# A memory-bound SwiGLU: the first tile loaded in three parts, and multiplied and stored in eight column pieces

## The chip, the cores and the metric

One core of a Trainium2 chip. The metric is the device time of the kernel in microseconds (us); lower is better. All runs quoted here were with the clock granted in full (1.00 in every one). A trace's span is some 1.8 us shorter than the time of its run. ACT is ScalarE, DVE VectorE; SP is SyncE, which here only issues transfers. A transfer (DMA) is cut into packets, here one for each contiguous row (in the kernel before 3968 loads of 64 KB and 3840 stores of 32 KB, besides those of the last two tiles), and 16 DMA engines carry them (16.0 packets are under way at a time, on the mean from 100 to 900 us). A transfer has landed when its last packet has arrived. "Packet records" are the start, length and size of each packet in a trace; sums over them are given for one engine, as the mean of the 16.

## The reference

```python
# x: 8192 x 8192 float32
a, b = np.split(x, 2, axis=-1)
return a * (b / (1 + np.exp(-b)))      # 8192 x 4096 float32
```

The input is 268.4 MB and the output 134.2 MB. All of it passes through the DMA engines once (402.67 MB in the trace of the kernel before).

## The kernel before

Two rows of x lie in one partition, so a tile is 128 partitions x 16384 floats (64 KB in each partition, 8 MB in all). There are 32 tiles and three buffers. ACT computes silu in place, DVE multiplies in place, and the product lies packed in the first half of the tile. SP issues the loads, ACT the stores, but those of the last two tiles are issued by SP.

```python
def load(i, rows=None):
    if i not in tiles:
        tiles[i] = pool.tile([P, R * M], x.dtype, name="xt")
    lo, hi = (0, R) if rows is None else rows
    nc.sync.dma_start(
        out=tiles[i][:, lo * M : hi * M], in_=xv[i * P : (i + 1) * P, lo * M : hi * M]
    )

def swiglu(i, k, c0=0, cw=half):
    xt = tiles[i]
    b = xt[:, k * M + half + c0 : k * M + half + c0 + cw]
    nc.scalar.activation(out=b, in_=b, func=_SILU)
    nc.vector.tensor_mul(out=xt[:, k * half + c0 : ...], in0=xt[:, k * M + c0 : ...], in1=b)

def store(i, c0=0, cw=R * half):
    (nc.scalar if i < last - 1 else nc.sync).dma_start(
        out=ov[i * P : (i + 1) * P, c0 : c0 + cw], in_=tiles[i][:, c0 : c0 + cw]
    )

for i in range(BUFS):            # 3
    load(i)
for i in range(last):            # 31
    for k in range(R):           # 2
        swiglu(i, k)
    if i == last - 1:
        swiglu(last, 0)
    store(i)
    nxt = i + BUFS
    if nxt < last:
        load(nxt)
    ...                          # the last tile: loaded, computed and stored by rows
```

## Time and profile before

| | before |
|---|---|
| time, median of 6 runs | 936.4 us (935.6 to 937.1) |
| span of the trace | 934.8 us |
| busy DVE, ACT | 30%, 25% |
| mean rate, whole span | 431 GB/s |
| mean rate, 100 to 900 us | 434 GB/s |
| load: issue to landing | 34.5 us |
| store: issue to landing | 39.7 us |
| period of a tile | 29.0 us |

A tile brings 8 MB in and 4 MB out, 12.58 MB in 29.0 us, which is the 434 GB/s. The compute engines idle for two thirds of the time and nothing is wrong with that: they are not the bound. The DMA engines are (9 tenths or more busy in 39 of 40 slices). The two landing times are longer than the 29 us period because each queue holds a little more than one transfer at a time (34.5/29.0 = 1.2 loads, 39.7/29.0 = 1.4 stores). Of a load's 34.5 us its own packets take 19.3 in each engine (8 x 2.418), of a store's 39.7 us 9.7 (8 x 1.213); the rest is time spent waiting in line.

In steady state the three buffers go round in a ring: load 34.5, compute 12.7, store 39.7, together 87 us, three periods.

### The profile page before, as it was taken

What the parts mean: (1) busy time and instruction counts of PE and PEld (TensorE: products, weight loads), DVE (VectorE), ACT (ScalarE), POOL (GpSimd) and SP (SyncE); (2) the same over time, 40 slices, a digit from 0 to 9 for tenths busy, and PEclk for the clock granted to TensorE, in tenths of its full rate; (3) what the DMA queues carried; (4) which work ended last, traced back from release to release, by engine and by line L of the source; (5) the groups of instructions that cost most, each with busy time, mean ns of one, the idle gap of its engine ahead of it and who ended that gap; (6) DMA issues with size and microseconds to landing.
All of it is one profiled execution on the core that took longest, in us unless ns stands there. A gap on an engine that the chain in (4) does not pass through costs nothing.

```text
span 934.8 us, 367 instructions
## 1 busy us (share of the span) xinstructions
DVE 283.3 (30%) x65; ACT 229.4 (25%) x66; POOL 0.2 (0%) x4
## 2 busy tenths in 40 slices
DVE  0333312333123331133321333213332133331242
ACT  0223320233302333113331133311333203332041
POOL 0000000000000000000000000000000000000000
DMA  9999999999999999999999999999999999999998
GB/s 404 400 445 430 430 439 433 428 435 443 428 430 439 429 442 432 435 426 453 419 430 452 411 452 423 428 447 425 433 433 453 414 443 429 426 447 428 425 437 376
DMA packets 9506, 402.67 MB, mean 431 GB/s; under 512 B 1056, under 2 KB 1056, under 8 KB 1056
## 3 DMA queue, kind: packets, MB, share of 16 engines
q1 hardware_dynamic: 5184, 276.83, 68.6%
q10 hardware_dynamic: 4320, 125.83, 31.2%
q14 instruction: 2, 0.02, 0.0%
HBM read 268.44 MB, written 134.22 MB: 431 GB/s over the span
## 4 chain that ended last, share of the span: by engine, by line
DMA 84%; DVE 10%; ACT 4%; DVEq 0%; issue 0%; SPq 0%; ACTq 0%
DMA out_dram<-xt 42%; DMA xt<-in_x_dram 42%; DVE xt L51 10%; ACT xt L50 4%; DVEq L106 0%; SPq L43 0%; ACTq L50 0%; DVEq L51 0%
## 5 line engine op out<-in xcount | busy, mean ns | idle before, releaser
L51 DVE TENSOR_TENSOR xt<-xt 128x4096 f32<-128x4096 f32 (+1 forms) x65 | 283.3, 4359 | 637.7 <-ACT xt L50 634.5
L50 ACT ACTIVATE xt<-xt 128x4096 f32<-128x4096 f32 (+1 forms) x65 | 228.1, 3556 | 688.1 <-DMA xt<-in_x_dram 688.1
L50 ACT ACT_TABLE_LOAD x1 | 1.3, 1283 | 0.7 <-PEq L95 0.7
L95 POOL MEMSET const-bfloat16-1.0<- 128x1 bf16 x1 | 0.1, 103 | 0.0
L95 POOL MEMSET const-uint8-127<- 128x1 uint8 x1 | 0.1, 102 | 0.0
L95 POOL MEMSET const-float32-0.0<- 128x1 f32 x1 | 0.1, 100 | 0.2 <-issue 0.2
L95 POOL MEMSET const-float32-1.0<- 128x1 f32 x1 | 0.1, 99 | 0.0
## 6 DMA issues: line engine op xcount, KB each, us to landing
out_dram<-xt ACTq DMA_DIRECT2D x30, 4096.0 KB, 39.7
xt<-in_x_dram SPq DMA_DIRECT2D x2, 4096.0 KB, 27.1
out_dram<-xt SPq DMA_DIRECT2D x1, 4096.0 KB, 23.6
out_dram<-xt SPq DMA_DIRECT2D x2, 2048.0 KB, 14.5
xt<-in_x_dram SPq DMA_DIRECT2D x31, 34.5
```

Of the source, the lines that this page charges most:

```text
L50: nc.scalar.activation(out=b, in_=b, func=_SILU)
L51: nc.vector.tensor_mul(out=xt[:, k * half + c0 : k * half + c0 + cw], in0=xt[:, k * M + c0 : k * M + c0 + cw], in1=b,)
L95: nc = _bacc.Bacc("TRN2", target_bir_lowering=False, num_devices=1)
```

## The change

Nothing is written in the first 35 us: the first tile has to arrive whole (it is there at 22.6 us) and be computed (12.6 us) before its store. The change loads tile 0 as a piece of 1024 columns of both halves of row 0 (1 MB), the rest of row 0 (3 MB) and row 1 (4 MB), and computes and stores it in eight pieces of 1024 columns.

```diff
+    def load_piece(i, k, c0, cw):
+        if i not in tiles:
+            tiles[i] = pool.tile([P, R * M], x.dtype, name="xt")
+        src = xv[i * P : (i + 1) * P, :].rearrange("p (k s c) -> p k s c", k=R, s=2)
+        dst = tiles[i].rearrange("p (k s c) -> p k s c", k=R, s=2)
+        nc.sync.dma_start(out=dst[:, k, :, c0 : c0 + cw], in_=src[:, k, :, c0 : c0 + cw])
...
-    for i in range(BUFS):
+    q = half // 4
+    load_piece(0, 0, 0, q)
+    load_piece(0, 0, q, half - q)
+    load(0, (1, 2))
+    for i in range(1, BUFS):
         load(i)
     for i in range(last):
+        step = q if i == 0 else half
         for k in range(R):
-            swiglu(i, k)
+            for c0 in range(0, half, step):
+                swiglu(i, k, c0, step)
+                if i == 0:
+                    store(i, k * half + c0, step)
         if i == last - 1:
             swiglu(last, 0)
-        store(i)
+        if i:
+            store(i)
```

## The prediction

> **What bounds the kernel now.** I read the page first: engine shares, then the 40 slices, then the queues.
>
> ```profile
> DVE 283.3 (30%) x65; ACT 229.4 (25%) x66; POOL 0.2 (0%) x4
> ...
> DMA  9999999999999999999999999999999999999998
> ...
> q1 hardware_dynamic: 5184, 276.83, 68.6%
> q10 hardware_dynamic: 4320, 125.83, 31.2%
> ...
> HBM read 268.44 MB, written 134.22 MB: 431 GB/s over the span
> ```
>
> No compute engine is busy for a third of the span, while the 16 DMA engines are at 9 tenths in every slice but the last. The two queues (q1: the loads and the last stores, issued by SP; q10: the other stores, issued by ACT) take 99.8% of the DMA time. So the limit is the bytes, 402.7 MB, and a change can help only by filling moments in which the DMA engines idle or run slowly. How many there are is read from the windows (columns: stretch, its length, DVE and ACT busy, POOL, clock, DMA share, GB/s):
>
> ```profile
> 22.00:36.00 14.00, 8.85 (x2) 7.12 (x2) 0.00 (x0) 1.00 0.93 403
> 36.00:60.00 24.00, 8.85 (x2) 7.12 (x2) 0.00 (x0) 1.00 1.05 429
> 60.00:100.00 40.00, 8.85 (x2) 7.12 (x2) 0.00 (x0) 1.00 0.97 422
> 100.00:500.00 400.00, 123.91 (x28) 99.72 (x28) 0.00 (x0) 1.00 1.00 435
> 500.00:900.00 400.00, 123.31 (x28) 99.72 (x28) 0.00 (x0) 1.00 1.00 433
> 900.00:932.00 32.00, 9.51 (x4) 7.33 (x3) 0.00 (x0) 1.00 0.99 428
> 932.00:935.00 3.00, 0.00 (x0) 0.00 (x0) 0.00 (x0) 1.00 0.07 27
> ```
>
> A packet here is a whole row of 64 or 32 KB and is counted in one piece, so windows of a few us are off by some per cent; long ones are good. From 100 to 900 us the mean is 434 GB/s, and 402.65 MB at that rate take 927.8 us. The span is 934.8, so only 7.0 us are lost in all. The window from 0 to 100 us has 418 GB/s: 16 GB/s too few for 100 us is 1.6 MB, or 3.7 us at 434. From 900 to 932 it is 6 GB/s x 32 us = 0.19 MB, 0.4 us; after 932 there is almost nothing, 2.8 us. **The whole of the start, which is all that the change touches, thus has 3.7 us to give, 0.4% of the time.** The packet records of the trace say what these are: the first packet starts 1.74 us into the span; the first packet of each engine takes about 3.1 us where a 64 KB packet later takes 2.42; and where the first store joins (36 to 42 us) one or two load packets of each engine take 3 to 4 us.
>
> The timeline shows when stores begin:
>
> ```profile
> 22.61 7.12 ACT L50 ACTIVATE xt<-xt 128x4096 f32<-128x4096 f32 x2 [20.60 <-DMA xt<-in_x_dram]
> 26.25 8.96 DVE L51 TENSOR_TENSOR xt<-xt 128x4096 f32<-128x4096 f32 x2 [26.25 <-ACT xt L50]
> 35.24 0.37 ACTq L58 DMA_DIRECT2D out_dram<-xt  x1
> ```
>
> Nothing is written before 35 us. It looks like waste and isn't: in that time loads of tiles 1 and 2 are already queued and keep the engines full. A 64 KB load packet takes 2.42 us both alone (10 to 35 us) and between stores (after 100 us): 27.1 GB/s an engine, 434 GB/s for 16. Reads alone run as fast as reads and writes mixed.
>
> [...] with both queues filled an engine takes one load packet (2.42 us) and one store packet (1.21 us) in turn, one round each 3.62 us. [...] The change's first load is 1 MiB and its first eight stores 0.5 MiB each; no transfer of this size is in the trace of before. The records do bound the fixed part: two 32 KB packets (2 x 1.213) against one of 64 KB (2.418) differ by 8 ns.
>
> **The change part by part.**
> Removed: one 8 MB load, four operations on 4096 columns and one 4 MB store, all of tile 0.
> Added: loads of 1 MB (16 packets of 4 KB an engine), 3 MB (16 of 12 KB) and 4 MB (8 of 32 KB); eight operations of 1024 columns on ACT and on DVE; eight stores of 8 packets of 4 KB. Bytes are the same. Packets an engine: 8 + 8 become 40 + 64, 88 more; at 8 ns that is 0.7 us. If they cost twice that, 1.4 us.
> ACT: from 3.61 us at 4096 and 1.90 at 2048 columns, 0.19 fixed + 0.855 per 1024, so 1.05 us a piece; DVE (4.425 and 2.288) 0.15 + 1.07 = 1.22 us. The order on ACT is silu, store, silu, store; a store waits for its multiply, so a piece takes about 2.4 us, eight take 19 instead of 12.6. Neither engine is the bound, so this is hidden.
> Moved, worked with packet times (about 0.16 us for 4 KB, 0.46 for 12 KB, 1.21 for 32 KB, 2.42 for 64 KB): the first piece has landed near 6 us, its store is issued near 8.3 instead of 35.2. The 3 MB piece lands near 14, store 1 is issued near 16.6. From here each 4 KB store packet waits behind a load packet: row 1 until about 24.5 us (1.37 us a round), then tile 1 (2.58 a round, 8 rounds, until 45), then tile 2 (until 66). Store 1 ends near 32, store 2 near 53, and at 66 some 35 small packets of tile 0's stores are left, which alone take 35 x 0.16 = 5.6 us, until about 71.5.
> The built program shows two waits made by the reuse of eight DMA semaphores: tile 2's load now waits for store 1 (near 33 us: 12 us before tile 1's load runs out, so no gap), and tile 1's store for store 2 (near 54, before its data are ready at 59). Tile 3's load waits for all eight stores, so it is issued near 73; before, it was at 69.9. In between, tile 1's store (issued near 59, queued behind the pieces) keeps the engines busy from 71.5. From 75 us loads and stores alternate as before.
> Sum: no DMA idle time removed except perhaps part of the 3.7 us, 0.7 to 1.4 us of packet overhead added, and the 1 to 1.5 us stall at the first store kept or had once more, since the store queue runs empty after store 0. Net: about +0.5 us.
>
> **The rivals.**
> (a) Overlap gain: stores begin 27 us earlier, and if those 27 us had been unused for writing, 27 us would be won at the end. Against it: the DMA share is 0.9 to 1.0 from the start and the rate is at its plateau; bytes written early only push back bytes read. It would give 910 us; I don't believe it. A small part of it, an end to the slow packets of the start, gives 933.
> (b) Starvation: tile 0's buffer comes free later because small packets lose every turn, the loads run dry at 66 us and SP waits until 73. For it: the rounds above. Against harm: while loads are missing, stores are queued (tile 0's rest, then 4 MB of tile 1), and the engines work on. Only if pieces of 4 KB ran at half speed alone would it cost: 8.4 MB touched by the change, 19 us at full rate, but only the 2.6 us of the first load and the 5.6 us of the rest stand alone: +8 us, 944. If the semaphore waits also opened a gap, 948.
> (c) Shifted phase at the end: with reads and writes displaced by some us, the last tile could find an emptier store queue, and its last multiply (landing 914.5, last store issued 921.0) would be exposed. The queues have slack: load 34.5 us and store 39.7 us to landing in a 29 us period. Worth 1 to 3 us at most.
>
> **Range and chances.** 936.4 + 0.5 gives 936.9; call it 937. Low 933.5: most of the 3.7 us recovered. High 941.5: half of rival (b). The 2% marks are 18.7 us off: a gain so large is five times what the start holds, a loss so large needs 8.1 MB worth of DMA idleness. Faster 0.005, same 0.97, slower 0.025.
>
> **What would show it.** Right: store issues from about 8 us on; the third 8 MB load (tile 3's) near 73 us; DMA 9 in all slices but the last, about 415 to 420 GB/s in the first 100 us; 434 after; tile 0's stores taking 15 to 45 us to landing though each is only 0.5 MB. Wrong: a slice of DMA under 9 between 60 and 80 us (b), a rate clearly over 434 in any long window (a), or a gap after 915 us (c).

The sum came to about +0.5 us (0.7 to 1.4 us of packets, less perhaps part of the 3.7 us): 936.9, called 937. No window of 400 us that was taken of these runs has more than 435 GB/s.

The packet times of the forecast, 0.16 us for 4 KB and 0.46 for 12 KB, are estimates from the 2.418 us of 64 KB and the 8 ns a packet; the trace of the changed kernel has 0.159 and 0.460. That a piece gets one packet's turn was an estimate too, from the turns in the trace of before (from 100 to 900 us, one load packet of an engine follows the last after 3.62 us in the median, and in 73% of the cases). The changed kernel shows it for the pieces: one 4 KB store packet and one 32 KB load packet in turn take 1.36 us, beside a 64 KB one 2.57. The eight semaphores are in both traces, the transfers land on eight. The half speed in rival (b) is an assumption; in e5_small_packets (below) 4 KB reads alone moved 370 to 393 GB/s from 10 to 40 us, not half of 434.

## The result, and the profile after

937.1 us (936.6 to 938.5, 6 runs) against 936.4: the ratio is 1.001 with a 95% interval of 0.9997 to 1.0023. A ratio here is the mean time of one kernel's fast runs over that of the other's fast runs of the same rounds, so it isn't quite the ratio of the medians. **The time did not change.** The stores did start early. The timeline of the changed kernel (start, length, engine, line, operation; the idle time before it in brackets):

```profile
6.42 1.06 ACT L58 ACTIVATE xt<-xt 128x1024 f32<-128x1024 f32 x1 [4.41 <-DMA xt<-in_x_dram]
7.50 1.23 DVE L59 TENSOR_TENSOR xt<-xt 128x1024 f32<-128x1024 f32 x1 [7.50 <-ACT xt L58]
8.76 0.37 ACTq L66 DMA_DIRECT2D out_dram<-xt  x1
...
36.35 0.34 ACTq L66 DMA_DIRECT2D out_dram<-xt  x1
46.51 7.12 ACT L58 ACTIVATE xt<-xt 128x4096 f32<-128x4096 f32 x2 [11.44 <-DMA xt<-in_x_dram]
...
68.13 7.12 ACT L58 ACTIVATE xt<-xt 128x4096 f32<-128x4096 f32 x2 [14.50 <-DMA xt<-in_x_dram]
```

The first store is issued at 8.8 us instead of 35.2 and the eighth at 36.4. Tile 1 is there at 46.5 us, as before (46.4). The windows of the changed kernel (stretch, length, DVE, ACT, POOL, clock, DMA share, GB/s):

```profile
0.00:100.00 100.00, 27.50 (x12) 23.98 (x13) 0.20 (x4) 1.00 0.99 418
100.00:500.00 400.00, 123.91 (x28) 99.72 (x28) 0.00 (x0) 1.00 1.00 435
500.00:900.00 400.00, 119.49 (x27) 99.71 (x28) 0.00 (x0) 1.00 1.00 433
```

The kernel before, for the first of these stretches:

```profile
0.00:100.00 100.00, 26.55 (x6) 22.65 (x7) 0.20 (x4) 1.00 0.99 418
```

Set beside the kernel before: 418 GB/s in the first 100 us in both, 435 and 433 after that in both. 26 us of earlier writing have moved not one more byte by the time 100 us have passed. What was written early was read later. Counted from the packet records, the kernel before has read 11.89 MB and written nothing at 30 us; the changed one has read 10.65 and written 0.82. At 100 us the sums are 41.62 and 41.50 MB.

What did change is in the page of the changed kernel, its chain and its issues (size, us from issue to landing):

```profile
DMA xt<-in_x_dram 49%; DMA out_dram<-xt 35%; DVE xt L59 10%; ACT xt L58 4%; DVEq L124 0%; SPq L51 0%; SPq L45 0%; ACTq L58 0%; DVEq L59 0%
...
out_dram<-xt ACTq DMA_DIRECT2D x29, 4096.0 KB, 32.3
...
out_dram<-xt ACTq DMA_DIRECT2D x8, 512.0 KB, 37.1
...
xt<-in_x_dram SPq DMA_DIRECT2D x30, 41.9
```

The issues of the kernel before, and of a version with a later first store (e6_store_later, below):

```profile
out_dram<-xt ACTq DMA_DIRECT2D x30, 4096.0 KB, 39.7
xt<-in_x_dram SPq DMA_DIRECT2D x31, 34.5
```

```profile
out_dram<-xt ACTq DMA_DIRECT2D x30, 4096.0 KB, 33.7
xt<-in_x_dram SPq DMA_DIRECT2D x31, 40.5
```

Before, the chain had 42% for each direction, loads took 34.5 us to landing and stores 39.7. Now loads take 41.9 and stores 32.3. The sum is 74.2 in both. In the changed kernel 7.4 us of waiting stand in the load queue and no longer in the store queue, for the whole rest of the run, and the period stayed 29 us. This isn't the mark of an early store: a first store that comes 7 or 19 us later (e3_store_late: loads 40.0, stores 34.3; e6_store_later: 40.5 and 33.7) or a split load alone (e1_load_split: 39.9 and 34.4) shifts it the same way, and the sum stays at 74.2 to 74.3. How the 74 us divide is decided somewhere at the start; what decides it, these runs don't settle, and no time goes with it. A reader who looked at the store alone would see a store that had become 19% faster, in a kernel that hadn't.

The 512 KB line is worth a look too: an eighth of a tile took as long to store (37.1 us) as a whole tile did (39.7 in the kernel before). Beside a filled load queue each small packet waited behind a large load packet (one 4 KB and one 64 KB packet in turn, 2.57 us a round, from 24 to 42 us), and each piece behind the pieces before it (they landed in order of issue, from 23.5 to 72.7 us). In c2_hold_change (below) four of the same pieces were issued when no load was queued; they landed in 2.6 to 2.9 us.

### The profile page after: what moved, and what is told of

Its sections match the earlier page's. It is cut to its first block, busy times and chain, and to the rows that moved or that the text cites. A ratio compares the mean times of both kernels' runs of the same rounds, so it can differ in the third digit from the quotient of the medians.

```text
span 936.7 us, 400 instructions
## 1 busy us (share of the span) xinstructions
DVE 284.2 (30%) x71; ACT 230.7 (25%) x72; POOL 0.2 (0%) x4
## 4 chain that ended last, share of the span: by engine, by line
DMA 84%; DVE 10%; ACT 4%; DVEq 0%; issue 0%; SPq 0%; ACTq 0%
DMA xt<-in_x_dram 49%; DMA out_dram<-xt 35%; DVE xt L59 10%; ACT xt L58 4%; DVEq L124 0%; SPq L51 0%; SPq L45 0%; ACTq L58 0%; DVEq L59 0%
## 5 line engine op out<-in xcount | busy, mean ns | idle before, releaser
L59 DVE TENSOR_TENSOR xt<-xt 128x4096 f32<-128x4096 f32 (+2 forms) x71 | 284.2, 4005 | 638.1 <-ACT xt L58 635.0
L58 ACT ACTIVATE xt<-xt 128x4096 f32<-128x4096 f32 (+2 forms) x71 | 229.5, 3273 | 688.2 <-DMA xt<-in_x_dram 679.8
## 6 DMA issues: line engine op xcount, KB each, us to landing
out_dram<-xt ACTq DMA_DIRECT2D x29, 4096.0 KB, 32.3
out_dram<-xt ACTq DMA_DIRECT2D x8, 512.0 KB, 37.1
xt<-in_x_dram SPq DMA_DIRECT2D x30, 41.9
```

The lines of the kernel that those rows point to most:

```text
L59: nc.vector.tensor_mul(out=xt[:, k * half + c0 : k * half + c0 + cw], in0=xt[:, k * M + c0 : k * M + c0 + cw], in1=b,)
```

## The experiments

The theory (A): the 16 DMA engines work without a hole from the first packet on, at one rate whether they read or write, so that the time is bytes over rate plus a start and an end; when writing starts doesn't matter. The rivals: (B) the early start gains something which the small pieces give back, so that the parts of the change alone would differ from 1 in opposite directions; (C) reading and writing overlap, so that the start of writing matters by itself.

| run | what | us | before, same rounds | ratio, 95% |
|---|---|---|---|---|
| e1_load_split | load split only | 936.6 | 936.3 | 1.0004 (0.9991 to 1.0016) |
| e2_store_split | store split only | 936.3 | 936.3 | 1.0000 (0.9987 to 1.0012) |
| e4_rows | the change in large pieces | 937.8 | 936.3 | 1.0018 (1.0005 to 1.0030) |
| e3_store_late | first store 7 us later | 936.4 | 936.3 | 1.0002 (0.9989 to 1.0016) |
| e6_store_later | first store 19 us later | 935.9 | 936.5 | 0.9993 (0.9977 to 1.0010) |
| c1_hold | a hole at the start | 956.4 | 936.5 | 1.0211 (1.0194 to 1.0228) |
| c2_hold_change | that hole, with the change | 948.0 | 936.5 | 1.0125 (1.0110 to 1.0140) |
| c3_hold_sp | a cleaner hole | 951.3 | 936.5 | 1.0159 (1.0142 to 1.0176) |
| c4_hold_sp_change | that hole, with the change | 937.8 | 936.5 | 1.0018 (1.0003 to 1.0033) |
| e5_small_packets | all packets 4 KB | 991.8 | 936.5 | 1.0601 (1.0576 to 1.0625) |
| f1_change_again | the change once more | 937.3 | 936.3 | 1.0011 (0.9997 to 1.0025) |

All gave correct results.

### The parts of the change, one by one

**e1_load_split**, against the changed kernel:

```diff
-        step = q if i == 0 else half
+        step = half
-                if i == 0:
-                    store(i, k * half + c0, step)
-        if i:
-            store(i)
+        store(i)
```

> Only the load of tile 0 is split (1 MB, 3 MB, 4 MB); it is computed in two halves of 4096 columns and stored whole, as before. Theory A (the DMA engines are busy from the first packet, so only packet overhead and stalls count): the store starts near 36 us as before, with its stall of 1.5 us; 40 load packets for 8 in each engine add about 0.25 us, slow small first packets 0.3 us: 936.4 + 0.5, ratio 1.000 to 1.002. Rival B (the early load gains time which the small stores give back): under 0.998.

**e2_store_split**, against the changed kernel:

```diff
-    load_piece(0, 0, 0, q)
-    load_piece(0, 0, q, half - q)
-    load(0, (1, 2))
-    for i in range(1, BUFS):
+    for i in range(BUFS):
         load(i)
```

> Tile 0 is loaded whole as before, but multiplied and stored in eight pieces from about 25 us. Theory A: 56 more store packets at 8 ns add 0.45 us, the stall where the first store joins may shrink from 1.5 to about 0.3 us as it did in the changed kernel: 935.5 to 937, ratio 0.999 to 1.001. Rival B (small stores cost several us, hidden in the changed kernel by a gain of the early start): 1.003 or more.

Measured: 1.0004 and 1.0000. Each part alone is worth nothing: neither the small loads nor the small stores cost anything that a gain would have to make good, at the level of 0.15% that these intervals resolve. Neither part has the whole early start, though (the first store is issued at 31.9 us in the first, at 25.1 in the second); the next run has it, without small packets.

**e4_rows**, against the changed kernel:

```diff
-    load_piece(0, 0, 0, q)
-    load_piece(0, 0, q, half - q)
+    load(0, (0, 1))
     load(0, (1, 2))
...
-        step = q if i == 0 else half
+        step = half
```

> The change with large pieces: tile 0 is loaded as two rows of 4 MB and stored as two rows of 2 MB, no packet under 16 KB (the store rows are 16 KB, the loads 32 KB). Theory A: packet overhead is under 0.15 us; the stores start near 22 us instead of 35, which gains nothing: 935.5 to 937, ratio 0.999 to 1.001. Rival B (an early start is worth something once the small packets are gone): under 0.996.

Measured: 937.8, 1.0018, so 0.8 us above the range I gave. Its first store is issued at 21.0 us, and it isn't faster, so rival B falls. But it is slower by 1.5 us without a small packet in it. At 900 us it is 0.25 MB (0.6 us) behind the kernel before. In its packet records the load packets from 24 to 36 us, where the stores join, took 1.1 us longer in each engine than the usual 2.42 us each, and those from 76 to 84 us, where loads start again after their queue had run empty, another 0.7 us. The kernel before has 1.5 us of the first kind, at 36 to 44 us, and none of the second; the changed kernel has 0.3 and 0.4. Why load packets are slow when one of the two queues starts, and why by so different amounts, these runs don't settle. Nor is the rest of the 1.5 us accounted for (0.4 of it lies after the last packet, 1.6 us before the span's end against 1.2 in the kernel before).

### The start of writing, moved the other way

**e3_store_late**, against the kernel before:

```diff
             swiglu(i, k)
         if i == last - 1:
             swiglu(last, 0)
+        if i == 0:
+            continue
+        if i == 1:
+            store(0)
+            load(BUFS)
         store(i)
```

> The opposite of the change: tile 0's store is issued only with tile 1's, near 59 us instead of 35. Theory A: reads fill the engines until 60 us, then two queued stores; tile 3's load waits for the first store, issued near 71 instead of 70: nothing lost, ratio 0.998 to 1.002. Rival C (the time at which writing starts matters, as reads and writes overlap): 24 us later costs up to 24 us, ratio 1.01 to 1.026.

The edit did less than I meant. Its timeline shows the store beside the first activation of tile 1, at 42.0 us, not at 59: the store waits for a multiply that was long done (at 35.3 us), and it was issued as the first of tile 1's two activations started.

```profile
42.01 3.62 ACT L50 ACTIVATE xt<-xt 128x4096 f32<-128x4096 f32 x1 [12.20 <-DMA xt<-in_x_dram]
42.01 0.37 ACTq L58 DMA_DIRECT2D out_dram<-xt  x1
```

So this is a delay of 6.8 us. Rival C would have it cost up to 0.7%; measured 1.0002 with an upper end of 1.0016. To make it larger, **e6_store_later** put tile 0's store behind tile 1's:

```diff
-        store(i)
+        if i == 0:
+            continue
+        if i == 1:
+            store(1)
+            store(0)
+            load(BUFS)
+        else:
+            store(i)
```

> Tile 0's store is issued behind tile 1's, near 55 us (the first attempt moved it only from 35 to 42, since ACT issued it beside the first activation of tile 1). Theory A: reads fill the engines until about 59 us, two stores from 56 to 78, tile 2's from 75: ratio 0.998 to 1.003. Rival C (the time at which writing starts matters): 20 us later, up to 1.021.

The timeline shows both stores together, 19 us later than the first store of the kernel before:

```profile
45.60 8.96 DVE L51 TENSOR_TENSOR xt<-xt 128x4096 f32<-128x4096 f32 x2 [10.37 <-ACT xt L50]
54.59 0.86 ACTq L58 DMA_DIRECT2D out_dram<-xt  x2
64.83 7.12 ACT L50 ACTIVATE xt<-xt 128x4096 f32<-128x4096 f32 x2 [15.75 <-DMA xt<-in_x_dram]
```

The time is 935.9 us, ratio 0.9993. Writing started at 9 us, at 35 or at 55 us, and the kernel took the same time (937.1, 936.4 and 935.9 us). Rival C falls. Meanwhile the reads run ahead: tile 2 is there at 64.8 us, 10.6 us earlier than in the kernel before (75.4).

### What would make the change pay

If A is right, the change must pay in a kernel whose DMA engines do idle at the start. So I made one: the loads of tiles 1 and 2 held back behind tile 0's store. **c1_hold**, against the kernel before (`load` gets an argument for the issuing engine):

```diff
-    for i in range(BUFS):
-        load(i)
+    load(0)
...
         store(i)
+        if i == 0:
+            load(1, eng=nc.scalar)
+            load(2, eng=nc.scalar)
```

> A control, the kernel before with an artificial hole: the loads of tiles 1 and 2 are issued by ACT behind tile 0's store, at about 36 us, so the DMA engines idle from about 22.5 to 37 us. Theory A (time follows the DMA engines' idle time): 14.5 us longer, 951, ratio 1.0155. Rival (there is slack in the three buffers that takes such a hole up): under 1.005.

**c2_hold_change** is the changed kernel with the same hold, the two loads issued by ACT behind the eight stores.

> The same hole with the change in it: tile 0 in pieces, tiles 1 and 2 loaded behind its eight stores. Theory A: by the time the loads are issued (about 37 us) 12.6 MB are through instead of 8.4, so 4.2 MB or 9.7 us of the hole are filled, less 0.8 us of packet overhead: 942 to 944, ratio 1.006 to 1.008 to before, some 8 us under the control. Rival (small stores run slowly or block the queue): no better than the control.

Measured: 956.4 and 948.0. The difference, 8.4 us, is what was expected, but both are some 5 us longer than expected. The windows of c1_hold say where:

```profile
22.00:37.00 15.00, 8.85 (x2) 7.12 (x2) 0.00 (x0) 1.00 0.08 35
37.00:96.00 59.00, 8.57 (x2) 7.12 (x2) 0.00 (x0) 1.00 1.02 435
96.00:150.00 54.00, 17.98 (x5) 15.68 (x5) 0.00 (x0) 1.00 0.95 385
```

There is the hole that I made, 35 GB/s from 22 to 37 us, and a second, 385 GB/s from 96 to 150: 49 GB/s too few for 54 us is 2.6 MB, or 6 us at 434 (5.4 us by the packet records). I made that one too, by mistake. Tile 3's load, issued by SP at 47 us, shared the engines with those of tiles 1 and 2 in ACT's queue and overtook tile 2's (its packets ended at 86 us, tile 2's at 106). Tile 1's store stood behind tile 2's load in ACT's queue and was through at 116 us. At that time tiles 2 and 3 were both still in compute, and nothing was queued until tile 4's load, issued at 116 us. By the packet records the engines idled for 2.0 us there; the other 3.4 us are load packets slower than 2.42 us around it (100 to 132 us). So I ran a control without the second queue.

**c3_hold_sp**, against the kernel before:

```diff
-        (nc.scalar if i < last - 1 else nc.sync).dma_start(
+        (nc.scalar if 0 < i < last - 1 else nc.sync).dma_start(
...
-    for i in range(BUFS):
-        load(i)
+    load(0)
...
         store(i)
+        if i == 0:
+            load(1)
+            load(2)
```

> The control once more, without the second hole that the loads in the other queue brought about (tile 3's load overtook those of tiles 1 and 2): tile 0's store is issued by SP and the loads of tiles 1 and 2 behind it, by SP too. Theory A: one hole, from 22.3 to about 36.5 us, and nothing else: 950.5 to 951.5, ratio 1.015 to 1.016. Rival (the first control lost 19.9 us because idle time at the start costs more than its own length): 1.02 or more.

**c4_hold_sp_change** is the changed kernel with the same edits.

> The same with the change in it: eight pieces, their stores and then the loads of tiles 1 and 2 issued by SP. ACT doesn't wait for stores here, so the loads are issued near 32 us, when 12.6 MB (29 us) are through: a hole of 1 to 3 us: 937.5 to 940, ratio 1.001 to 1.004, and 11 to 13 us under the control. So the change would be worth over 1% in a kernel whose DMA engines idle at the start. Rival (small pieces are no use even there): within 3 us of the control.

Measured: 951.3 and 937.8. Here are the windows of c3_hold_sp and of c4_hold_sp_change from 22 us on:

```profile
22.00:37.00 15.00, 8.85 (x2) 7.12 (x2) 0.00 (x0) 1.00 0.08 35
37.00:100.00 63.00, 15.30 (x4) 14.25 (x4) 0.00 (x0) 1.00 1.00 418
100.00:500.00 400.00, 117.46 (x27) 96.02 (x27) 0.00 (x0) 1.00 1.00 434
```

```profile
22.00:37.00 15.00, 4.63 (x4) 3.90 (x4) 0.00 (x0) 1.00 1.07 424
37.00:100.00 63.00, 17.70 (x4) 14.24 (x4) 0.00 (x0) 1.00 0.99 421
100.00:500.00 400.00, 123.89 (x28) 99.72 (x28) 0.00 (x0) 1.00 1.00 433
```

In the first, the hole: 35 GB/s for 15 us. At 434 that is 15 x (1 - 35/434) = 13.8 us of work not done, and the kernel is 14.7 us longer. In the second, the pieces fill the hole (424 GB/s) and the time is back within 1.3 us of the kernel before. **The very change that is worth nothing in the real kernel is worth 13.5 us in this one.** The difference between the two isn't in the change but in whether the loads of tiles 1 and 2 are queued already.

### The price of small packets

**e5_small_packets**, against the kernel before; every load and store becomes two, of alternating chunks of 1024 columns, so that no two chunks join to a longer row:

```diff
+    def copy(eng, dst, src):
+        d, s = (ap.rearrange("p (a b c) -> p a b c", b=2, c=1024) for ap in (dst, src))
+        for b in range(2):
+            eng.dma_start(out=d[:, :, b, :], in_=s[:, :, b, :])
```

> The suspected packet cost made large: every load and store of the kernel before is cut so that each packet is 4 KB (two DMAs of alternating 1024-column chunks for each one). Theory A with 8 ns a packet: in each engine 32 x 120 more load packets and 32 x 56 more store packets, 5632 x 8 ns = 45 us: 981, ratio 1.048. Rival (the small packets of the changed kernel were cheap only because there were few[...]): over 1.10. Rival (packets cost nothing, the changed kernel's 0.75 us has another cause): under 1.01.

(The reason that the first rival gave is cut: no trace shows it.)

Measured: 991.8, ratio 1.060, 55 us longer; I expected 45. The windows:

```profile
20.00:30.00 10.00, 0.00 (x0) 2.25 (x2) 0.00 (x0) 1.00 1.02 370
30.00:40.00 10.00, 7.22 (x2) 6.15 (x2) 0.00 (x0) 1.00 1.01 377
40.00:50.00 10.00, 1.63 (x1) 0.00 (x0) 0.00 (x0) 1.00 0.99 355
...
500.00:900.00 400.00, 120.30 (x28) 92.59 (x26) 0.00 (x0) 1.00 1.02 419
```

With reads and writes mixed the rate is 419 GB/s. Over all bytes, 402.65/419 against 402.65/433 is 31 us, less than my 45: a 4 KB packet is recorded with 159 ns, 7.9 more than a sixteenth of a 64 KB packet, but the records of neighbours overlap a little, and the DMA share stands at 1.02. The other 24 us are load packets slower than 159 ns, and by the packet records nearly all of them (23 us) had no store packet within 0.3 us. Most fall in the first 350 us: load packets with no store packet within 1 us take 172 to 201 ns on the mean there (each stretch of 50 us taken by itself), and 162 ns later (from 350 to 360 us loads alone move 414 GB/s). So the size per packet was about right, but for another reason in part: small reads alone were dearer than small reads beside writes, much so early in the run. Why early, these runs don't show. Since the changed kernel has 80 packets of 4 KB in each engine, of which only the first 16 (the 1 MB load, 211 ns on the mean) run as reads alone, it pays under 2 us for them: an estimate from these figures is 16 x 60 ns (211 against the 151 of a sixteenth of a 64 KB packet) and 64 x 8 ns, 1.5 us.

### The 0.75 us

> The changed kernel itself once more, to see whether its 0.75 us are real and where they lie. Theory A: at 100 us it is 0.1 MB (0.3 us) behind the kernel before, as in its first trace, and the rest of the difference is how evenly the 16 engines end[...]: ratio 1.0000 to 1.0010 and an interval that holds 1. Rival (a steady loss of more than packets explain): 1.0010 or more, clear of 1.

(Cut from it is a figure for how much the ends vary from run to run, which isn't shown. In the first traces of the two kernels the 16 engines end within 1.8 us of each other before, 931.8 to 933.6 us, and within 2.9 in the changed kernel, 932.1 to 935.0.)

Measured: 937.3 against 936.3, 1.0011 (0.9997 to 1.0025), so the ratio is just above the range I gave; in the trace the kernel is 0.16 MB (0.4 us) behind at 100 us, as before by 0.12, and still 0.17 at 900 us. The mean end of the last 16 packets comes 0.4 us later too. That half is accounted for by the packet records up to 100 us (first trace of the changed kernel, each engine): 0.75 us more for small packets and 0.25 for the slow ones of the first 8 us, less 0.75 because load packets lose less where a queue starts (0.3 us from 8 to 12 us and 0.4 from 76 to 88; before, 1.5 from 36 to 44). That leaves 0.25 us, or 0.1 MB. The other half lies after the last packets: from the last packet to the end of the span it is 1.7 to 1.8 us in both traces of the changed kernel and 1.2 in that of before. But c4_hold_sp_change, which has the same pieces, has 1.3, and e4_rows, with large pieces, 1.6, so it doesn't go with the small pieces, and what it comes from isn't shown. The intervals of both comparisons hold 1, but both lie mostly above it: a loss of 0.1% is neither shown nor excluded.

No version beat both kernels: the fastest, e6_store_later, has an interval that holds 1.

## Why the prediction was right

It gave 937.0 us, and 937.1 came.

- **"The whole of the start ... has 3.7 us to give."** Confirmed: 418 GB/s in the first 100 us before and after; six runs of other starts without a hole, the repeat among them, lie between 0.9993 and 1.0018.
- **"Reads alone run as fast as reads and writes mixed."** This is the step on which all rests. Shown for rows of 64 KB by e6_store_later, which reads alone for 19 us more and loses nothing (load packets of 2.42 us, no idle time from 12 to 40 us). Writing alone is as fast for rows of 32 KB: in c1_hold only tile 1's store runs from 106 to 116 us, at 1.21 us a packet as elsewhere. For rows of 4 KB reads alone were slower (e5_small_packets), but the change has too few of them to matter.
- **Packets.** 0.7 to 1.4 us of overhead were expected, net +0.5 after the stalls; 0.3 to 0.4 us are in the traces at 100 us. That the net came so near is partly luck. The overhead is there (0.75 us, and 0.25 for slow first packets), but the stall, which the prediction kept or had once more at 1 to 1.5 us, fell to 0.7 in two parts; and about half of the difference in f1_change_again's trace lies after the last packets, where nothing was forecast.
- **The time table of the pieces.** First store at 8.3 (came 8.8), store 1 at 16.6 (17.2), tile 1 there at about 46 (46.5), tile 3's load near 73 (73.0). One date was wrong: store 1 was to end near 32 us and release tile 2's load at 33. The load was issued at 42.9, when store 1 had landed (42.86), and that was 1.4 to 3 us before tile 1's last packets ended (44.3 to 45.9 us, by engine), not 12. I had let store 0 enter the engines 1.2 us after its issue; its first packet came 3.7 us after it (12.4; in the kernel before it was 4.2 us for the first engine, and 0.87 us in c1_hold, where the engines were idle: store issued at 35.20 us, first packet at 36.07), and store 1's packets waited behind it until 22 us. So "no gap" was wrong for the load queue: tile 2's first packets came 3.6 us after the issue (46.5), and for 2 us on the mean an engine had no load. It cost nothing because store packets were waiting: 131 small ones start between 44 and 46 us, against 5 to 16 in each 2 us from 30 to 44, and the engines are busy throughout.
- **Rival (a), the gain from overlap:** refuted by e3, e6 and the windows. **Rival (b), starvation:** the pieces did wait long (37.1 us for 512 KB), and the engines worked on with other packets meanwhile, as argued. The loads did run dry, from 67 to 77 us (expected: dry at 66, the next load issued at 73), and small stores, then tile 1's, filled those 10 us; no slice of the page is under 9 but the last. c1_hold shows what it looks like when both queues do run dry (315 GB/s from 110 to 120 us). **Rival (c), the shifted phase:** it came about, 7.4 us moved from the store queue to the load queue and stayed there, and the whole change cost under 1 us. But e1, e2, e3, e4 and e6 show a shift of 5 to 6 us too, so it isn't special to the early stores.

## What to carry to other kernels

Before moving a transfer earlier, ask what the DMA engines do at that moment. Here they were busy (a share of 0.99 in the first 100 us), and the early stores only pushed back loads (41.50 MB moved at 100 us, 41.62 before), however bad the engine timelines looked. In c3_hold_sp they idled (0.08 from 22 to 37 us), and the same edit gave back 13.5 of 14.7 us. The test costs a glance: in this kernel the rate in the first 100 us against the rate in the middle (418 and 434 GB/s), times the length, left the start 3.7 us to give, and no other start without a hole gained more than 0.1%.
